# An RMS norm that streams 64 MB: three rows stored singly between pieces of a load, statistics one group ahead, and bulk transfers cut by partition

## The chip, the cores and the metric

The kernel runs on one core of a Trainium2 chip. A core has engines that work side by side: VectorE (DVE), ScalarE (ACT), TensorE (PE), GpSimd (POOL) and SyncE (SP), which here does nothing but issue transfers. Transfers between the chip's main memory (HBM) and the on-chip memory of 128 partitions (SBUF) are carried by 16 DMA engines. The metric is the time of one execution on the device in microseconds; the median over several runs is compared.

## The reference

The input `x` is 16 x 1024 rows of 512 fp32 numbers, 16,384 rows in all; `gamma` has 512 numbers.

```python
rms = np.sqrt(np.mean(x ** 2, axis=-1, keepdims=True) + 1e-5)
return (x / rms * gamma).astype(np.float32)
```

Every row is squared and averaged, and the row is then scaled by one number of its own and by `gamma`. So 33.5 MB are read and 33.5 MB are written, with little arithmetic for each number.

## The kernel before

The 16,384 rows are four tiles of 128 partitions x 32 rows x 512 numbers, 8 MB each (1 MB is 2^20 bytes in this text where tiles are spoken of; a tile is 64 KB in each partition). Row r of a tile in a partition lies beside row r+1 in HBM, so a partition's 32 rows are one contiguous piece. Three tiles fit in SBUF, as `slot0`, `slot1` and `slot2`. The fourth tile goes into `slot0` again, once the first tile has been stored from it. The results are written over the input in the slot and stored from there.

All large transfers are issued from SP in the order of the program: `load` is line 42 and `store` line 45. Each is one transfer over all 128 partitions. SP works through its list in order. Where a transfer must wait (a store for the arithmetic, a load for the store that frees its slot), SP waits, and all that stands behind it on SP waits too. Transfers that have been issued then stand in the queue of the DMA engines.

`compute` works on groups of eight rows (G = 8). There are two ways to get the sums of squares. In even groups ScalarE squares one row at a time and accumulates its sum (line 78, eight times). In odd groups ScalarE squares four rows at a time into PSUM (line 72) and VectorE sums these (line 73). Then ScalarE takes the root of eight means (line 84), VectorE the reciprocal (line 85), and VectorE scales each of the eight rows by its own number and by `gamma` (line 87). The order in which these instructions stand on each engine is made by a scheduler from the program, which mixes neighbouring groups.

The order of transfers on SP (lines 47 to 49, and lines 96 to 112): the first tile in two loads of 16 rows, the second tile in one load, then one single row of the first tile as a store, then the third tile in one load, the other 31 rows of the first tile, half of the second tile, the two halves of the fourth tile as loads into `slot0`, the other half of the second tile, the third tile, and the two halves of the fourth tile. The single-row store makes the load behind it on SP wait until that row has been computed.

Of the kernel before, what the change touches and what calls it, by code (L numbers as in the profile page):

```python
# [1 line left out]

# [4 lines left out]


@with_exitstack
def kernel(  # L10
    ctx: ExitStack,
    tc: tile.TileContext,
    x: bass.AP,
    gamma: bass.AP,
    out: bass.AP,
):
    nc = tc.nc
    P = nc.NUM_PARTITIONS
    eps = 1e-5
    fp32 = mybir.dt.float32  # L20
    AF = mybir.ActivationFunctionType
    OP = mybir.AluOpType

    xf = x.flatten_outer_dims()
    of = out.flatten_outer_dims()
    N, D = xf.shape
    R = 32
    G = 8
    H = 4
    assert N == 4 * P * R  # L30

    xv = xf.rearrange("(t p r) d -> t p r d", p=P, r=R)
    ov = of.rearrange("(t p r) d -> t p r d", p=P, r=R)

    const = ctx.enter_context(tc.tile_pool(name="const", bufs=1))
    stats = ctx.enter_context(tc.tile_pool(name="stats", bufs=4))
    psum = ctx.enter_context(tc.tile_pool(name="psum", bufs=2, space=bass.MemoryType.PSUM))

    slots = [const.tile([P, R, D], fp32, name=f"slot{i}") for i in range(3)]

    def load(t, slot, r0, r1):
        nc.sync.dma_start(out=slots[slot][:, r0:r1], in_=xv[t][:, r0:r1])

    def store(t, slot, r0, r1):
        nc.sync.dma_start(out=ov[t][:, r0:r1], in_=slots[slot][:, r0:r1])

    load(0, 0, 0, 16)
    load(0, 0, 16, 32)
    load(1, 1, 0, 32)

    gamma_row = const.tile([1, D], fp32)
    nc.scalar.dma_start(out=gamma_row, in_=gamma.unsqueeze(0))
    ones_col = const.tile([1, P], fp32)
    nc.vector.memset(ones_col, 1.0)  # L54
    gamma_psum = psum.tile([P, H, D], fp32, name="sq")
    nc.tensor.matmul(gamma_psum[:, 0], ones_col, gamma_row, start=True, stop=True)  # L56
    gamma_b = const.tile([P, D], fp32)
    nc.vector.tensor_copy(out=gamma_b, in_=gamma_psum[:, 0])  # L58

    eps_t = const.tile([P, 1], fp32)  # L60
    nc.vector.memset(eps_t, eps)  # L61
    sq_scratch = const.tile([P, D], fp32)

    def compute(slot, r0, r1):
        for g in range(r0, r1, G):
            ss = stats.tile([P, G], fp32, name="ss")
            rms = stats.tile([P, G], fp32, name="rms")
            rstd = stats.tile([P, G], fp32, name="rstd")
            if (g // G) % 2:
                for h in range(0, G, H):  # L70
                    sq = psum.tile([P, H, D], fp32, name="sq")
                    nc.scalar.activation(out=sq, in_=slots[slot][:, g + h : g + h + H, :], func=AF.Square)  # L72
                    nc.vector.tensor_reduce(  # L73
                        out=ss[:, h : h + H], in_=sq, axis=mybir.AxisListType.X, op=OP.add
                    )
            else:
                for r in range(G):
                    nc.scalar.activation(  # L78
                        out=sq_scratch,
                        in_=slots[slot][:, g + r, :],  # L80
                        func=AF.Square,
                        accum_out=ss[:, r : r + 1],
                    )
            nc.scalar.activation(out=rms, in_=ss, func=AF.Sqrt, bias=eps_t, scale=1.0 / D)  # L84
            nc.vector.reciprocal(out=rstd, in_=rms)  # L85
            for r in range(G):
                nc.vector.scalar_tensor_tensor(  # L87
                    out=slots[slot][:, g + r, :],
                    in0=slots[slot][:, g + r, :],
                    scalar=rstd[:, r : r + 1],  # L90
                    in1=gamma_b,
                    op0=OP.mult,
                    op1=OP.mult,
                )

    compute(0, 0, 8)
    store(0, 0, 0, 1)
    load(2, 2, 0, 32)
    compute(0, 8, 32)
    store(0, 0, 1, 32)  # L100
    compute(1, 0, 16)
    store(1, 1, 0, 16)
    load(3, 0, 0, 16)
    load(3, 0, 16, 32)
    compute(1, 16, 32)
    store(1, 1, 16, 32)
    compute(2, 0, 32)
    store(2, 2, 0, 32)
    compute(0, 0, 16)
    store(3, 0, 0, 16)  # L110
    compute(0, 16, 32)
    store(3, 0, 16, 32)


# [1 line left out]
_INS = ['x', 'gamma']  # L116
_OUTS = [((16, 1024, 512), 'float32')]


# [23 lines left out]
```

## Time and profile before

| What | Value |
|---|---|
| Median of 11 runs | 162.19 us (161.86 to 162.61) |
| The profiled execution's own time | 162.1 us |
| Its span (first to last instruction) | 160.3 us |
| VectorE busy | 123.4 us (77%), 163 instructions |
| ScalarE busy | 79.9 us (50%), 162 instructions |
| Scaling of rows, line 87 | 128 instructions, 744 ns each, 85.7 us |
| Sums from PSUM, line 73 | 16 instructions, 2274 ns each, 36.1 us |
| Squares by four rows, line 72 | 16 instructions, 1860 ns each, 29.8 us |
| Squares by one row, line 78 | 64 instructions, 625 ns each, 40.0 us |
| HBM read and written | 33.56 MB and 33.55 MB |

The page gives each engine's busy time, a row of 40 slices of the span with a digit for the busy share in tenths, the packets of each DMA queue with the time that they took as a share of 16 engines' span, the chain of work that ended last, and the waits. In an answer on waits the numbers are the total in microseconds, how often, and the longest. In the timeline the first number is the start in microseconds, the second the duration of the instruction; for an instruction that issues a transfer this is the issue alone. In an answer on DMA issues the last number is the median of the microseconds from issue to landing; where the answer covers one issue, it is that issue's own.

### The profile page before, as it was taken

To read this page: it belongs to the slowest core of one execution; us is meant where nothing else is said; L and a number is where in the kernel's file an instruction comes from. 1 tells how busy PE (TensorE), PEld (TensorE's weight loads), DVE (VectorE), ACT (ScalarE), POOL (GpSimd) and SP (SyncE) were. 2 spreads that over 40 slices of the span, in tenths; PEclk is the share of its full clock that TensorE was granted. 3 is DMA by queue.
4 is the path that set the end of the run, shared out by engine and by line. 5 is a ranking of instruction groups with operands and counts; after the bars stand their busy time and mean duration, and the time that the engine had idled before them with its cause. 6 is when DMAs were issued, how large, how long until landed. Compare 5 with 4: busy or idle time off the path is not lost.

```text
span 160.3 us, 404 instructions
## 1 busy us (share of the span) xinstructions
PE 2.0 (1%) x2; PEld 0.5 (0%) x2; DVE 123.4 (77%) x163; ACT 79.9 (50%) x162; POOL 0.2 (0%) x4
## 2 busy tenths in 40 slices
PE   4000000000000000000000000000000000000000
PEld 1000000000000000000000000000000000000000
DVE  0101909999999509999999999998999999998000
ACT  3008999930490999993089504002998970000000
POOL 0000000000000000000000000000000000000000
DMA  7999999969799895999899999999997997999993
GB/s 262 392 401 491 417 392 523 523 262 523 327 525 425 360 523 253 509 507 412 348 392 499 409 401 474 433 401 442 450 531 343 458 507 327 433 425 401 392 507 147
DMA packets 1876, 67.13 MB, mean 419 GB/s; under 512 B 209, under 2 KB 209, under 8 KB 338
## 3 DMA queue, kind: packets, MB, share of 16 engines
q1 hardware_dynamic: 1872, 67.11, 97.8%
q14 instruction: 2, 0.02, 0.0%
q10 hardware_dynamic: 2, 0.00, 0.0%
HBM read 33.56 MB, written 33.55 MB: 419 GB/s over the span
## 4 chain that ended last, share of the span: by engine, by line
DVE 71%; ACT 12%; DMA 8%; issue 1%; DVEq 0%
DVE slot L87 52%; DVE ss L73 18%; DMA slot<-in_x_dram 8%; ACT sq_scratch L78 6%; ACT sq L72 4%; DVE rstd L85 1%; ACT L84 1%; ACT rms L84 1%; DVEq L138 0%
## 5 line engine op out<-in xcount | busy, mean ns | idle before, releaser
L87 DVE SCALAR_TENSOR_TENSOR slot<-slot,rstd,gamma_b 128x512 f32<-128x512 f32 x128 | 85.7, 744 | 0.1
L78 ACT ACTIVATE sq_scratch<-slot 128x512 f32<-128x512 f32 x64 | 40.0, 625 | 14.4 <-DMA slot<-in_x_dram 13.0
L73 DVE TENSOR_REDUCE ss<-sq 128x4 f32<-128x2048 f32 x16 | 36.1, 2274 | 10.5 <-ACT sq L72 10.4
L72 ACT ACTIVATE sq<-slot 128x2048 f32<-128x2048 f32 x16 | 29.8, 1860 | 4.4 <-DVE ss L73 4.4
L84 ACT ACTIVATE rms<-ss,eps_t 128x8 f32<-128x8 f32 x16 | 4.4, 297 | 37.4 <-DVE ss L73 37.2
L78 ACT ACTIVATION_READ_ACCUMULATOR sq_scratch<-slot 128x1 f32 x64 | 11.9, 186 | 0.0
L85 DVE RECIPROCAL rstd<-rms 128x8 f32<-128x8 f32 x16 | 2.7, 187 | 9.8 <-ACT rms L84 9.8
L58 DVE COPY gamma_b<-sq 128x512 f32<-128x512 f32 x1 | 0.7, 691 | 3.2 <-PE sq L56 3.2
L56 PE MATMUL sq<-gamma_row,ones_col 1*128 1x512 f32 x2 | 2.0, 1122 | 2.1 <-DMA gamma_row<-in_gamma_dram 2.1
L78 ACT ACT_TABLE_LOAD x1 | 1.3, 1283 | 1.3 <-PEq L127 1.3
L84 ACT ACT_TABLE_LOAD x1 | 1.3, 1283 | 0.0
L54 DVE MEMSET ones_col<- 1x128 f32 x1 | 0.2, 165 | 0.8 <-PEq L127 0.8
L56 PEld LDWEIGHTS sq<-gamma_row,ones_col 1*128 1x128 f32 x2 | 0.5, 308 | 2.1 <-issue 2.1
L127 POOL MEMSET const-bfloat16-1.0<- 128x1 bf16 x1 | 0.1, 102 | 0.0
L127 POOL MEMSET const-uint8-127<- 128x1 uint8 x1 | 0.1, 102 | 0.0
L127 POOL MEMSET const-float32-0.0<- 128x1 f32 x1 | 0.1, 99 | 0.2 <-issue 0.2
L127 POOL MEMSET const-float32-1.0<- 128x1 f32 x1 | 0.1, 99 | 0.0
L61 DVE MEMSET eps_t<- 128x1 f32 x1 | 0.1, 59 | 0.0
## 6 DMA issues: line engine op xcount, KB each, us to landing
slot<-in_x_dram SPq DMA_DIRECT2D x4, 4096.0 KB, 21.3
out_dram<-slot SPq DMA_DIRECT2D x4, 4096.0 KB, 17.8
out_dram<-slot SPq DMA_DIRECT2D x1, 7936.0 KB, 31.6
out_dram<-slot SPq DMA_DIRECT2D x1, 256.0 KB, 18.2
slot<-in_x_dram SPq DMA_DIRECT2D x2, 39.0
gamma_row<-in_gamma_dram ACTq DMA_DIRECT2D x1, 2.0 KB
out_dram<-slot SPq DMA_DIRECT2D x1, 23.0
```

Source lines behind the costliest of these rows:

```text
L54: nc.vector.memset(ones_col, 1.0)
L56: nc.tensor.matmul(gamma_psum[:, 0], ones_col, gamma_row, start=True, stop=True)
L58: nc.vector.tensor_copy(out=gamma_b, in_=gamma_psum[:, 0])
L61: nc.vector.memset(eps_t, eps)
L72: nc.scalar.activation(out=sq, in_=slots[slot][:, g + h : g + h + H, :], func=AF.Square)
L73: nc.vector.tensor_reduce(out=ss[:, h : h + H], in_=sq, axis=mybir.AxisListType.X, op=OP.add)
L78: nc.scalar.activation(out=sq_scratch, in_=slots[slot][:, g + r, :], func=AF.Square, accum_out=ss[:, r : r + 1],)
L84: nc.scalar.activation(out=rms, in_=ss, func=AF.Sqrt, bias=eps_t, scale=1.0 / D)
L85: nc.vector.reciprocal(out=rstd, in_=rms)
L87: nc.vector.scalar_tensor_tensor(out=slots[slot][:, g + r, :], in0=slots[slot][:, g + r, :], scalar=rstd[:, r : r + 1], in1=gamma_b, op0=O ...
L127: nc = _bacc.Bacc("TRN2", target_bir_lowering=False, num_devices=1)
```

## The change

The transfers are cut in other pieces, and the arithmetic is put in another order.

- The first tile's first load of 16 rows becomes two loads of 8.
- `load` and `store` get an argument `parts`, which cuts a transfer into consecutive ranges of partitions, issued one after the other. The second tile's load and the first tile's large store are cut in two (64 partitions each), the third tile's store in four (32 partitions each).
- The load of the third tile, which came in one piece behind the single-row store, now comes in three pieces (16, 8 and 8 rows), with a store of one more single row of the first tile between each two. The large store of the first tile begins at row 3.
- `compute` is divided into `row_stats` (squares, sums, root, reciprocal) and `apply` (scaling). The loop calls `row_stats` of the next group before `apply` of this one.

```diff
-    def load(t, slot, r0, r1):
-        nc.sync.dma_start(out=slots[slot][:, r0:r1], in_=xv[t][:, r0:r1])
+    def load(t, slot, r0, r1, parts=1):
+        for p in range(0, P, P // parts):
+            q = slice(p, p + P // parts)
+            nc.sync.dma_start(out=slots[slot][q, r0:r1], in_=xv[t][q, r0:r1])
...
+    def store(t, slot, r0, r1, parts=1):
+        for p in range(0, P, P // parts):
+            q = slice(p, p + P // parts)
+            nc.sync.dma_start(out=ov[t][q, r0:r1], in_=slots[slot][q, r0:r1])
...
-    load(0, 0, 0, 16)
+    load(0, 0, 0, 8)
+    load(0, 0, 8, 16)
     load(0, 0, 16, 32)
-    load(1, 1, 0, 32)
+    load(1, 1, 0, 32, parts=2)
...
+    def transfers(t, g):
+        if (t, g) == (0, 0):
+            store(0, 0, 0, 1)
+            load(2, 2, 0, 16)
+            store(0, 0, 1, 2)
+            load(2, 2, 16, 24)
+            store(0, 0, 2, 3)
+            load(2, 2, 24, 32)
+        elif (t, g) == (0, 24):
+            store(0, 0, 3, 32, parts=2)
+        elif (t, g) == (1, 8):
+            store(1, 1, 0, 16)
+            load(3, 0, 0, 16)
+            load(3, 0, 16, 32)
+        elif (t, g) == (1, 24):
+            store(1, 1, 16, 32)
+        elif (t, g) == (2, 24):
+            store(2, 2, 0, 32, parts=4)
+        elif (t, g) == (3, 8):
+            store(3, 0, 0, 16)
+        elif (t, g) == (3, 24):
+            store(3, 0, 16, 32)
+
+    ahead = row_stats(0, 0)
+    for k, (t, g) in enumerate(groups):
+        rstd = ahead
+        if k + 1 < len(groups):
+            tn, gn = groups[k + 1]
+            ahead = row_stats(slot_of[tn], gn)
+        apply(slot_of[t], g, rstd)
+        transfers(t, g)
```

## The prediction

> **What bounds the kernel now.** I read the page's chain first, then the DMA rows and the queue totals, then the waits of SP, and last the time of issue and the landing of each transfer.
>
> ```profile
> DVE 71%; ACT 12%; DMA 8%; issue 1%; DVEq 0%
> DMA  7999999969799895999899999999997997999993
> DMA packets 1876, 67.13 MB, mean 419 GB/s; under 512 B 209, under 2 KB 209, under 8 KB 338
> q1 hardware_dynamic: 1872, 67.11, 97.8%
> SPq L45 <- DVE slot L87: 122.4, 7, 28.3
> SPq L42 <- DMA out_dram<-slot: 8.2, 1, 8.2
> ```
>
> The chain puts 71% on VectorE, but the packets of SP's queue occupy 97.8% of sixteen DMA engines' span. Both can't be the bound. SP's waits for VectorE, 122.4 us in seven places, only delay the time at which a store joins the queue. Whether that costs anything is decided by what the queue still holds then. So here are five transfers with issue time (timeline) and time from issue to landing (DMA issues, asked around each issue):
>
> ```profile
> 25.23 0.44 SPq L42 DMA_DIRECT2D slot<-in_x_dram  x1
> 50.08 0.34 SPq L45 DMA_DIRECT2D out_dram<-slot  x1
> 117.02 0.34 SPq L45 DMA_DIRECT2D out_dram<-slot  x1
> 132.58 0.33 SPq L45 DMA_DIRECT2D out_dram<-slot  x1
> 147.88 0.33 SPq L45 DMA_DIRECT2D out_dram<-slot  x1
> ```
>
> ```profile
> slot<-in_x_dram SPq DMA_DIRECT2D x1, 37.4
> out_dram<-slot SPq DMA_DIRECT2D x1, 7936.0 KB, 31.6
> out_dram<-slot SPq DMA_DIRECT2D x1, 23.0
> out_dram<-slot SPq DMA_DIRECT2D x1, 4096.0 KB, 17.1
> out_dram<-slot SPq DMA_DIRECT2D x1, 4096.0 KB, 11.5
> ```
>
> Row by row: 25.23+37.4 = 62.6 is the landing of the third tile's load; 50.08+31.6 = 81.7 of the first tile's store; 117.02+23.0 = 140.0 of the third tile's store; 132.58+17.1 = 149.7 and 147.88+11.5 = 159.4 of the fourth tile's stores. The same sum for the others gives 12.8 and 22.5 (first tile), 42.3 (second tile, issued 1.64, 40.7 later), 43.0 (the single row, issued 24.84), 91.5 and 120.7 (second tile's stores) and 111.0 (fourth tile's load). Neighbouring landings differ by what a transfer needs at the rate of the bulk: 19.8, 19.6, 19.1, 19.3 us for 8 MB (the third is 7.75 MB), 9.7 us for 4 MB. And each store was issued before the queue had come to it: 50.08 against 62.6 (12.5 us spare), 117.02 against 120.7 (3.7), 147.88 against 149.7 (1.8). The queue is never empty. The kernel is bound by the DMA engines; VectorE, with 123.4 us busy, is second and has slack everywhere. The chain names it because that last store waited for it, without showing the 1.8 us of queue behind it.
>
> What can be won is small. The slope of 19.3 us for 8 MB over 64 MB is 154.4 us. The span has 160.3. The other 5.9 us are the start (the first 4 MB land at 12.8, 9.7 of it slope), the last 0.9 us after 159.4, and less than 2 us at changes of direction and the single row.
>
> [...] The trace of before agrees with the full rate: 8 MB in 19.3 us is 435 GB/s. It has no bulk transfer of fewer than 128 partitions, so the half rate isn't shown[...].
>
> **The change part by part.** Arithmetic first: 128 scalar_tensor_tensor, 16 tensor_reduce, 16 reciprocals, all squares and roots are the same in number and shape; only their order moves. Cost 0, hidden behind the queue.
>
> First load in parts: the first 8 rows (2 MB) land at about 8.0 instead of 12.8, as the first 4 MB took 9.7 us. ScalarE needed 12.81 to 22.14 for the eight row squares and two large squares ahead of the root, then the first row was out at 24.84. With an earlier start by 4.8 us it is out near 20. Its store isn't due before the second tile has landed, at 42.3, so nothing is gained. One more DMA issue on SP, 0.4 us at the start, comes after transfers that already run: 0.
>
> Statistics one group ahead: VectorE reduces the next group before it scales this one. The group that pays is the last one scaled before a store, at most two reduces (2 x 2274 ns) later, 4.5 us; after the queue has fallen behind as below, every store has more spare time than that. Cost 0. If the queue kept its rate, the stores with 3.7 and 1.8 us spare would be the ones to watch, but a group that is put ahead also has its reduces done when its own scaling starts, so the end of VectorE's total doesn't move.
>
> Three rows stored singly, between three pieces of the third tile's load: the single row now takes 42.3 to 43.0, 0.7 us, against 19.1/31 = 0.62 in bulk. Two more rows leave the bulk, 2 x 0.08, and there are four more changes of direction, bounded by 0.35 us at 62.6 to 81.7 (19.1 against 31 x 0.604 = 18.7). Bounds 0.1 to 1.4; I take 0.3. On SP the pieces wait behind row 1 and row 2, each 0.7 us of VectorE later, some 20 us before they are due. The waits for reused DMA semaphores name the first loads (landed by 22.5) and, for the two halves of the first store, the halves of the second tile's load. These land before the third tile's load begins, so the halves are still in the queue early: 0.
>
> The split by partition is the part that decides. Three bulk transfers lose half their partitions: the second tile's load (22.5 to 42.3: 19.8 us, now two of 64), the first tile's store without three rows (29/31 of 19.1 = 17.9, two of 64) and the third tile's store (120.7 to 140.0: 19.3, four of 32). Queue order puts the halves one after the other[...]. Lower bound: each packet keeps its rate, extra 0 (a gain is looked at below). Upper bound: exactly half the rate, extra 57.0. [...] I take 54.5[...].
>
> Is there cover for it? No: the queue is full from start to end. Does anything late add to it? The second tile lands near 61 (22.5 + 2 x 19.4), the third near 83, the first store ends near 118, only then are the two loads of the fourth tile issued, behind 9.7 us of the second tile's first store, which was ready at about 82 (the tile's landing plus some 20 us, half a tile's arithmetic and a wait): covered. Those loads land near 138 and 148, the second tile's other store near 157, the third tile's store near 195, the last two near 205 and 215. VectorE needs 123.4/4 = 31 us per tile: third tile ready at about 130, due at 157; fourth about 166, due at 205. No new hole.
>
> Sum against the profiled execution: 160.3 + 54.5 + 0.3 = 215.1 us of span; the run of this profile took 162.1, 1.8 more than its span and 0.1 under the median 162.19. So 216.9, taken as **217.0 us**.
>
> **Rivals.** First, the split costs nothing[...]. Then span 160.3 + 0.3, time 162.4 (162.1 to 163.5). For it: no transfer of before has fewer partitions, so nothing in the profile excludes it. [...]
>
> Second, only one direction is limited, loads (write to SBUF) or stores: 162.1 + 19.8 + 0.3 = 182.2, or 162.1 + 37.2 + 0.3 = 199.6. Engines drifting apart, so that some are in the other half already, would land between these too. Against it: landings follow each other as one queue, and no row of before tells the directions apart.
>
> Third, it gets faster. Place: the end of each transfer[...]. It needs the half rate to be absent and the row cost near its lower bound. The price is in the less than 2 us of changes; half of it is 0.8 us, time 161.4. It decides from 0.4 us of gain onward, more than the rows take. Against: nothing in the page shows an engine waiting.
>
> **How the numbers follow.** Half rate both ways 0.72 (212 to 221), one direction or drift 0.10 (182 to 210), no cost 0.14, faster 0.04. Of the 0.14, 0.06 lie within 0.2% (161.87 to 162.51, about what a measurement of this kernel tells from no change) and 0.08 above. So faster 0.04, same 0.06, slower 0.90. The range from 180 to 222 leaves out the last two cases, 0.18.
>
> **What would show it.** Right: packets of SP's queue 15 x 128 + 2 x 64 + 2 x 64 + 4 x 32 and 16 small ones for each of 23 transfers, 2672 in all (before: 13 x 128 + 13 x 16 = 1872); their time still near 97% of the engines; the GB/s row near 215 in three stretches (22 to 61, 83 to 118, 157 to 195) and near 430 elsewhere; landings as listed; mean near 312 GB/s. Half rate wrong: no slow stretch, second tile at 42.3. One direction: one or two of the three. Hole: a DMA digit well under 9 inside the span, and a store issued later than the landing ahead of it. What makes the forecast wrong above all is the split of 64 rows over the engines, of which before shows nothing.

## The result, and the profile after

The changed kernel takes 221.33 us (median of 12 runs, 220.01 to 223.54) against 162.30 us for the kernel before (46 runs). The ratio is 1.3626, with a 95% interval from 1.3599 to 1.3653; ratios in this text leave out executions more than 1.5% above the fastest of their kernel, here one of the twelve. The profiled execution took 220.04 us with a span of 218.3 us, 58.0 us more than before.

First the page of the changed kernel: the DMA rows in 40 slices of 5.5 us, the packets, and SP's queue.

```profile
span 218.3 us, 425 instructions
DMA  6999999999969999889995999999999899979993
GB/s 250 432 471 420 348 192 192 192 192 192 192 276 446 393 431 486 174 174 261 218 218 252 420 354 408 450 396 426 474 276 204 192 252 192 216 204 426 426 432 144
DMA packets 2676, 67.13 MB, mean 308 GB/s; under 512 B 369, under 2 KB 369, under 8 KB 754
q1 hardware_dynamic: 2672, 67.11, 97.8%
```

The DMA engines are as busy as before, 97.8% of the span, with the same 67.11 MB. There is no hole that would explain 58 us. But in three stretches, slices 6 to 11, 17 to 22 and 31 to 36, the second row shows about 200 GB/s where the rest shows about 430. A busy share alone hides this: it is 97.8% here as before, at 308 GB/s for 419, since an engine counts as busy for the whole of a packet, however slowly the packet moves. Bytes and busy share must be read together.

The packets show it more sharply. These are the totals of SP's queue in a stretch of the second tile's load: before from 24 to 41 us, then after from 25 to 60 us, each with packets of 64 KB (after has 16 of a few bytes beside them). The columns are packets, MB, and time of the packets as a share of 16 engines' stretch; a packet's whole time counts where it starts, so a share can pass 100%.

```profile
q1 hardware_dynamic: 112, 7.34, 102.3%
```

```profile
q1 hardware_dynamic: 128, 7.34, 101.9%
```

Before, 112 large packets take 1.023 x 16 x 17 us, 2.48 us each (2.42 once such a load is under way, as a cut of it shows below). After, the same 112 packets and 7.34 MB take 1.019 x 16 x 35 us, 5.1 us each. The work on the queue is the same; each packet takes a little more than twice as long.

Next the issue times of the changed kernel's transfers (timeline of SP, asked around each), and the time from issue to landing in the same order. In the first fence the first row holds five issues, of which the two halves of the second tile's load are the last.

```profile
0.72 2.56 SPq L44 DMA_DIRECT2D slot<-in_x_dram  x5
45.85 0.51 SPq L49 DMA_DIRECT2D out_dram<-slot  x1
63.32 0.50 SPq L49 DMA_DIRECT2D out_dram<-slot  x1
160.22 0.35 SPq L49 DMA_DIRECT2D out_dram<-slot  x1
175.36 0.35 SPq L49 DMA_DIRECT2D out_dram<-slot  x1
```

```profile
slot<-in_x_dram SPq DMA_DIRECT2D x1, 60.6
out_dram<-slot SPq DMA_DIRECT2D x1, 3712.0 KB, 54.6
out_dram<-slot SPq DMA_DIRECT2D x1, 3712.0 KB, 55.7
out_dram<-slot SPq DMA_DIRECT2D x1, 4096.0 KB, 47.5
out_dram<-slot SPq DMA_DIRECT2D x1, 4096.0 KB, 42.1
```

The second half of the second tile's load, issued at 2.7, lands at 63.3; the halves of the first tile's store at 100.4 and 119.0; the last two stores at 207.8 and 217.4. Each of the last two stores takes over 40 us from issue to landing, of which 9.6 us are the transfer itself (217.4 - 207.8); the kernel before had 11.5 us for the last one. The arithmetic is now far from the end of the span. From differences of landings, on both sides counted to the last engine's:

| Stretch of the queue | Before, us | After, us | More |
|---|---|---|---|
| up to the first tile's landing | 22.5 | 23.0 | 0.5 |
| second tile's load (split in 2) | 19.8 | 40.3 | 20.5 |
| single rows and third tile's load | 20.3 | 22.1 | 1.8 |
| rest of the first tile's store (split in 2; two rows less) | 19.1 | 33.6 | 14.5 |
| second tile's stores, fourth tile's loads | 39.0 | 40.4 | 1.4 |
| third tile's store (split in 4) | 19.3 | 38.7 | 19.4 |
| fourth tile's stores | 19.4 | 19.3 | -0.1 |
| sum | 159.4 | 217.4 | 58.0 |

Two rows moved from the fourth line to the third, some 1.2 us. Then the three split transfers hold 20.5 + 15.7 + 19.4 = 55.6 us of the 58.0.

The chain of waits misleads here too. For the changed kernel it begins so:

```profile
another core or an unknown queue 26%; DVE 24%; ACT 16%; DMA 13%; issue 1%; DVEq 0%; SPq 0%; ACTq 0%
```

There is one core, and its queue is known. SP's own waits are of more use: its stores waited 46.4 us for loads (10.7 before), and the end of the program 41.5 us for stores (11.0 before). First the two lines of the kernel before, then those of the changed kernel:

```profile
SPq L138 <- DMA out_dram<-slot: 11.0, 2, 9.6
SPq L45 <- DMA slot<-in_x_dram: 10.7, 1, 10.7
```

```profile
SPq L49 <- DVE slot L94: 74.1, 5, 25.6
SPq L49 <- DMA slot<-in_x_dram: 46.4, 4, 19.8
SPq L162 <- DMA out_dram<-slot: 41.5, 5, 10.3
SPq L44 <- DMA out_dram<-slot: 29.1, 2, 18.5
```

### The profile page after: what moved, and what is told of

It reads as the page before. It is cut to its first block, busy times and chain, and to the rows that moved or that the text cites. A ratio compares the mean times of both kernels' runs of the same rounds, so it can differ in the third digit from the quotient of the medians.

```text
span 218.3 us, 425 instructions
## 1 busy us (share of the span) xinstructions
PE 2.0 (1%) x2; PEld 0.5 (0%) x2; DVE 123.1 (56%) x163; ACT 80.1 (37%) x162; POOL 0.2 (0%) x4
## 3 DMA queue, kind: packets, MB, share of 16 engines
q1 hardware_dynamic: 2672, 67.11, 97.8%
## 4 chain that ended last, share of the span: by engine, by line
another core or an unknown queue 26%; DVE 24%; ACT 16%; DMA 13%; issue 1%; DVEq 0%; SPq 0%; ACTq 0%
DVE slot L94 19%; DMA slot<-in_x_dram 13%; ACT sq_scratch L82 9%; ACT sq L76 6%; DVE ss L77 5%; DVE rstd L89 1%; ACT rms L88 1%; DVEq L162 0%; SPq L49 0%; SPq L44 0%; ACTq L82 0%
```

## The experiments

Theory, from the prediction: a transfer that names only one half of the partitions (0 to 63 or 64 to 127, or 32 of these) moves at about half the rate, in both directions. This was an estimate of the author's, as no transfer of before is of this kind; in the changed kernel such packets took 5.1 us for 2.48. The traces show packets, bytes and times, but not what slows a packet, so the theory is tested by which partitions a transfer names. Rivals: the order of work opens holes; any transfer with fewer rows is slow; one direction alone is; the limit lies on the side of HBM, since half a tile's partitions are also half a tile's addresses.

### Which part of the change costs

**The changed kernel without the split.**

```diff
-    load(1, 1, 0, 32, parts=2)
+    load(1, 1, 0, 32)
...
-            store(0, 0, 3, 32, parts=2)
+            store(0, 0, 3, 32)
...
-            store(2, 2, 0, 32, parts=4)
+            store(2, 2, 0, 32)
```

> The changed kernel with every transfer over all 128 partitions again; the rows between the load's pieces, the first load in parts and the statistics one group ahead stay. [...]the split carries nearly all of the 59 us, so 163.2 us (162.4 to 164.0); what is left over is about 0.5 us for two more single rows and 0.5 us for the start. Rival (order of work: statistics ahead or the waits on SP for reused semaphores open holes in the queue): over 167 us, and a DMA digit under 9 inside the span.

162.36 us against 162.04, ratio 1.0023 (1.0014 to 1.0031), just under the range expected. So the split carries 221.33 - 162.36 = 59.0 us, and all the rest of the change 0.3. The queue's share is 97.7%, and no slice inside the span falls lower than in before. The order of work is out as a cause of the loss.

**The rows alone, on the kernel before.**

```diff
     store(0, 0, 0, 1)
-    load(2, 2, 0, 32)
+    load(2, 2, 0, 16)
+    store(0, 0, 1, 2)
+    load(2, 2, 16, 24)
+    store(0, 0, 2, 3)
+    load(2, 2, 24, 32)
...
-    store(0, 0, 1, 32)
+    store(0, 0, 3, 32)
```

> The kernel before with the three single rows between three pieces of the third tile's load, and nothing else. Theory: two more rows of 2 KB packets and four more changes of direction cost 0.5 us, time 162.8 (162.4 to 163.4). Rival (hidden: the rows would have been stored anyway): within 0.1 us of before. Rival (SP issues the pieces late, and the queue runs dry): over 164.

162.07 against 162.00, ratio 1.0000 (0.9989 to 1.0012), under the range expected: the rival "hidden" was right, and 0.5 us was too much. The rows don't slow the queue by anything that can be measured.

**First load in parts and statistics ahead alone**: the changed kernel with the split undone as above, and the rows too.

```diff
             store(0, 0, 0, 1)
-            load(2, 2, 0, 16)
-            store(0, 0, 1, 2)
-            load(2, 2, 16, 24)
-            store(0, 0, 2, 3)
-            load(2, 2, 24, 32)
+            load(2, 2, 0, 32)
...
-            store(0, 0, 3, 32)
+            store(0, 0, 1, 32)
```

> The changed kernel without the split by partition and without the two further rows: what is left is the first load in two parts and the statistics one group ahead. Theory: both hidden by the full queue, 162.3 (162.0 to 162.8), at most 0.5 us more at the start. Rival (the arithmetic's order matters at the end, where the last store had 1.8 us to spare): the last store is issued after 149.7 us of the span, and the time is over 163.

162.19 against 162.00, ratio 1.0004 (0.9993 to 1.0015). The trace shows what happened to the arithmetic:

```profile
20.58 0.35 SPq L49 DMA_DIRECT2D out_dram<-slot  x1
...
83.25 59.67 SPq L49 DMA_DIRECT2D out_dram<-slot  x4
```

The first row is out at 20.58 instead of 24.84, and the last store is issued at the end of the second row, 83.25 + 59.67 = 142.9, instead of 148.2 (both are the end of the issue). So the results are ready earlier, by 4 us at the start and 5 at the end, and all of it is spent waiting in the queue.

**The kernel before without its single row.**

```diff
-    store(0, 0, 0, 1)
     load(2, 2, 0, 32)
...
-    store(0, 0, 1, 32)
+    store(0, 0, 0, 32)
```

> The kernel before without its single-row store: the first tile is stored in one transfer of 32 rows, and the third tile's load is issued at the start. Theory: one row less in small packets and two changes of direction less save 0.1 to 0.5 us, time 162.0 (161.7 to 162.2). Rival: the queue moves the same bytes and nothing changes, 162.3.

A miss: 162.60 against 162.00, ratio 1.0036 (1.0022 to 1.0051). The loss is small but clear of the noise, and a gain or nothing was expected. There are fewer transfers and the same bytes, but the third tile's store and the last one take longer to land, 23.8 us for 23.0 and 12.3 for 11.5, from issue times within 0.1 us of before's. The third tile's load, now directly behind the second's, is where the spread between the sixteen engines first grows (landings from 61.8 to 63.1, in before from 62.2 to 62.6). Why an engine falls behind there isn't settled.

### One transfer split, one direction at a time

In this section and the next ones `load` and `store` have an argument `cuts`, the list of partitions between which a transfer is cut; its definition is left out of the diffs.

**The second tile's load in two halves.**

```diff
...
-    load(1, 1, 0, 32)
+    load(1, 1, 0, 32, cuts=(0, 64, 128))
```

> The kernel before with the second tile's load alone as two transfers of 64 partitions. [...]both halves at half rate, packets of 64 KB about 5.1 us instead of 2.42, the load 40.3 us instead of 19.8, time 162.3 + 20.5 = 182.8 (181 to 184). Rival stores only (writing to SBUF isn't limited): 162.5. Rival drift (the long run loses more or less because engines fall out of step): 175 to 180.

182.65 against 162.04, ratio 1.1266 (1.1247 to 1.1284): 20.6 us more, as expected.

**The third tile's store in four quarters.**

```diff
...
-    store(2, 2, 0, 32)
+    store(2, 2, 0, 32, cuts=(0, 32, 64, 96, 128))
```

> The kernel before with the third tile's store alone as four transfers of 32 partitions. [...]the store takes 38.7 us instead of 19.3, time 162.3 + 19.4 = 181.7 (180 to 183). Rival loads only: 162.5. Rival that the number of partitions sets the rate (32 of 128 is a quarter): 57 us more, 219.

183.24 against 162.04, ratio 1.1302 (1.1278 to 1.1325): 21.2 us more, just above the range expected. So both directions are limited, and cuts of 32 partitions cost what cuts of 64 do (21.2 us more on a store of 19.3, 20.6 on a load of 19.8). That the rate goes with the number of partitions as such is out: it would have cost 57 us.

### Fewer rows, or the wrong rows

**The load cut at 32 and 96.**

```diff
...
-    load(1, 1, 0, 32)
+    load(1, 1, 0, 32, cuts=(0, 32, 96, 128))
```

> The kernel before with the second tile's load as partitions 0 to 31, 32 to 95 and 96 to 127. The middle one has 64 partitions and the same packets as a half of the changed kernel, but 32 of each side of partition 64. [...]the middle transfer runs at the full rate, packets of 2.42 us, 9.7 us; the outer ones at half, 2 packets of 5.1 us per engine each, 10.2 us; together 30.1 instead of 19.8, time 172.6 (171.5 to 174). Rival (any transfer of 64 partitions or fewer is slow, by the number of its partitions or its shorter list for each engine): all three at half, 40 us, time 182.8, and no packets of 2.42 us in that stretch.

171.94 against 162.04, ratio 1.0602 (1.0586 to 1.0619), 9.9 us more. The three parts of the load in this kernel, issued at 1.62, 2.10 and 2.72 us, with their time to landing:

```profile
slot<-in_x_dram SPq DMA_DIRECT2D x1, 31.3
slot<-in_x_dram SPq DMA_DIRECT2D x1, 40.9
slot<-in_x_dram SPq DMA_DIRECT2D x1, 50.2
```

They land at 32.9, 43.0 and 52.9, after the first tile at 22.6. So 32 partitions (2 MB) take 10.3 us, the middle 64 (4 MB) 10.1, and 32 again 9.9. The queue's total from 33.5 to 41 us, inside the middle part, has 48 large packets and nothing else:

```profile
q1 hardware_dynamic: 48, 3.15, 96.8%
```

0.968 x 16 x 7.5 us / 48 = 2.42 us each. The transfer of partitions 32 to 95 runs at the full rate, and each neighbour of half its size takes as long. Which partitions, not how many: the rival of fewer rows is out.

**Even and odd partitions.**

```diff
-    load(1, 1, 0, 32)
+    for p in range(2):
+        nc.sync.dma_start(out=slots[1][p:P:2], in_=xv[1][p:P:2])
```

> The kernel before with the second tile's load as two transfers of 64 partitions, even ones and odd ones. [...]half rate, 182.8 (178 to 184). Rival [...]162.5. In between, 165 to 178, if the engines fall out of step and stay so.

161.93 against 162.00, ratio 0.9993 (0.9982 to 1.0004). The half rate, named first, fell; its rival was right: 64 partitions ran at the rate of 128 when every second one was named. The engines had not fallen out of step: in the DMA row from 24 to 41 us, in 40 slices of 0.425 us, the packets start together about every 2.4 us.

```profile
DMA  9700099000099000097000990000990000990000
```

Why this cut costs nothing isn't shown. The eight transfers of 16 partitions below test whether only the half counts in which the partitions lie. The run also shows that two transfers of 64 partitions cost nothing as such.

### Which side of the transfer

**One half of SBUF, addresses all over the tile in HBM.**

```diff
-    load(1, 1, 0, 32)
+    nc.sync.dma_start(out=slots[1][0:64], in_=xv[1][0:P:2])
+    nc.sync.dma_start(out=slots[1][64:128], in_=xv[1][1:P:2])
...
-    store(2, 2, 0, 32)
+    nc.sync.dma_start(out=ov[2][0:P:2], in_=slots[2][0:64])
+    nc.sync.dma_start(out=ov[2][1:P:2], in_=slots[2][64:128])
```

> The kernel before with the second tile's load and the third tile's store each in two transfers: SBUF partitions 0 to 63 with the even 64 KB blocks of the tile in HBM, 64 to 127 with the odd ones. (The rows of these two tiles so land in other places of the output; the work is the same.) Each transfer has one half of SBUF's partitions and addresses from all over the tile in HBM. Theory SBUF side: half rate in both, 20.3 and 19.4 us more, 202 (199 to 205). Rival HBM side (in the changed kernel a half is also a contiguous half of 8 MB of HBM): 162.5. If the load is limited on one side and the store on the other: about 182.

203.44 against 162.07, ratio 1.2557 (1.2530 to 1.2584): 41.4 us more, in the range of the theory.

**Both halves of SBUF, one half of the tile's addresses in HBM.**

```diff
-    load(1, 1, 0, 32)
+    nc.sync.dma_start(out=slots[1][0:P:2], in_=xv[1][0:64])
+    nc.sync.dma_start(out=slots[1][1:P:2], in_=xv[1][64:128])
...
-    store(2, 2, 0, 32)
+    nc.sync.dma_start(out=ov[2][0:64], in_=slots[2][0:P:2])
+    nc.sync.dma_start(out=ov[2][64:128], in_=slots[2][1:P:2])
```

> The counterpart: the same two tiles in two transfers each, even SBUF partitions with the first contiguous 4 MB of the tile in HBM, odd ones with the second. (Again the rows of these tiles land elsewhere.) Theory SBUF side: 162.3, packets of 2.42 us throughout. Rival HBM side: 202. One side for the load and the other for the store: about 182.

162.23 against 162.07, ratio 1.0010 (0.9998 to 1.0022). The queue's totals in the load, of the first kernel from 25 to 60 us, of the second from 24 to 41 us:

```profile
q1 hardware_dynamic: 128, 7.34, 102.0%
```

```profile
q1 hardware_dynamic: 128, 7.34, 100.5%
```

The same 7.34 MB need 35 us in the one and 17 us in the other. The limit is on the side of SBUF, for the load and for the store (one of them alone would have left some 182 us in both kernels). HBM is out.

### A half, or a smaller part

**Eight transfers of 16 partitions**, for the second tile's load and the third tile's store.

```diff
...
-    load(1, 1, 0, 32)
+    load(1, 1, 0, 32, cuts=range(0, 129, 16))
...
-    store(2, 2, 0, 32)
+    store(2, 2, 0, 32, cuts=range(0, 129, 16))
```

> The kernel before with the second tile's load and the third tile's store each in eight transfers of 16 partitions. [...]a quarter of the rate, 8 MB in some 78 us instead of 19.5, 58 us more for each of the two, 279 (265 to 290), packets near 10 us. Rival halves (only the side of partition 64 counts, as the even-odd cut[...] ran at full rate): 20 us more for each, 202, packets of 5.1 us.

260.61 (median of four, 258.1 to 262.7) against 162.07. The ratio, 1.5940 (1.5896 to 1.5983), is that of the two runs near 258 us; the trace is of the longest, 262.7. The total was outside the range named (265 to 290), but it is far from the rival's 202. The load does what was expected; the queue from 24 to 94 us:

```profile
DMA packets 224, 7.34 MB, mean 105 GB/s; under 512 B 112, under 2 KB 112, under 8 KB 112
q1 hardware_dynamic: 224, 7.34, 93.5%
```

112 large packets, 0.935 x 16 x 70 us / 112 = 9.35 us each, nearly four times the 2.42. The load takes 74.5 us (landings 23.2 to 97.7) for 19.8. So there is more than a half at work: 16 partitions in a row get about a quarter of the rate. With that, a limit that knows only two halves is out; how the even and odd partitions escape it stays open. The store takes 65.3 us instead of 77 (landings 175.2 to 240.5). In its landing events the first of the sixteen engines has finished the eighth part at 204.1 us and the last at 240.5: engines fall out of step, and those ahead are already in other parts. Its packets begin at 7 to 9.4 us each and later range from 2.4 to 13. Its 12 us under 77 are most of the 18 us by which the expectation was too high.

**Two halves at the same time from two lists.**

```diff
-    store(2, 2, 0, 32)
+    nc.sync.dma_start(out=ov[2][0:64], in_=slots[2][0:64])
+    nc.scalar.dma_start(out=ov[2][64:128], in_=slots[2][64:128])
```

> The kernel before with the third tile's store in two halves of 64 partitions, the first issued from SP, the second from ScalarE, at the same time. [...]nearly the half rate, 178 to 182. Rival out of step: [...]162 to 170; ScalarE's wait ahead of its transfer may then delay the fourth tile's squares by some 6 us, of which the queue has 7 to spare for the next store.

175.22 against 162.07, between both expectations. The four times, from 172.05 to 177.91, lie too far apart for a ratio. In the profiled execution (172.05 us) the issues around 117 us have this time to landing:

```profile
out_dram<-slot SPq DMA_DIRECT2D x1, 33.0
out_dram<-slot ACTq DMA_DIRECT2D x1, 33.1
```

The queue of ScalarE from 117 to 150 us:

```profile
q10 hardware_dynamic: 80, 4.19, 37.0%
```

Its 64 large packets (the other 16 are of a few bytes) take 0.370 x 16 x 33 us / 64 = 3.05 us each, between the 2.42 of the full rate and the 5.1 of a half. Issued at 117.1, both transfers land near 150.1. In before the single transfer landed at 140.0. Ten microseconds are lost instead of nineteen, and the queue is not empty before the last stores (landings 159.7 and 169.4; the last was issued at 157.4). Why these packets are slowed less than those of one half alone isn't shown. An uncut transfer is better by 10 to 16 us of the whole.

## Why the prediction was right

The forecast was 217.0 us with a range from 180 to 222; 221.33 was measured, near the upper end.

**The bound.** That the queue, not VectorE, sets the time was right. The clearest proof is the kernel without the split and the rows: its arithmetic was done 5 us earlier and its time was 1.0004 of before's.

**The split.** The forecast held in each point that the runs test: about half the rate for one half of the partitions (packets of 5.1 us), both directions (20.6 us more for the load alone, 21.2 for the store alone), one half after the other (the load's halves landed at 43.1 and 63.3), and no cover. What the partitions of a half have in common was not shown. The size was off by little. The step took 54.5 us, the author's estimate, a little under exact halving (57.0); no trace of before shows it. Of the profile's 58.0 us, 55.6 lie in the split transfers. Exact halving was no upper bound for the load: 40.3 us is 2.04 times 19.8, since a packet takes 5.1 us where twice 2.42 would be 4.84. The estimate had taken 54.5 / 57.0 = 0.96 of halving, and the load has 20.5 / 19.8 = 1.04. The store of the first tile was cheaper than halving, 15.7 for 17.9 us. Its packets (58 KB) show where. From 101.3 to 110.5 us, in the second half, 32 of them and nothing else give 1.006 x 16 x 9.2 / 32 = 4.63 us each:

```profile
q1 hardware_dynamic: 32, 1.90, 100.6%
```

But each engine's first packet, started from 83.3 to 84.9 us directly behind the third tile's load, took only 2.2 to 2.4 us. This alone saves 2.4 us on each engine; why these packets were not slowed isn't known. So the total came close to the forecast in part by luck: the load took 0.7 us more than halving and this store 2.2 us less, and neither was foreseen.

**The rest of the gap.** 218.3 of span against 215.1 is 3.2 us: 1.1 in the split transfers (55.6 for 54.5), 1.4 in the stretch behind the first store, and the rest at the start and the rows, where 0.3 was taken and 0.5 + 0.6 - 0.1 was read. The 1.4 us lie in packets of 32 KB, some of which took up to 2.4 us instead of 1.21, nearly all of them between 124 and 131 us and between 144 and 147, near the changes from store to load and back; the cause is open. Another 1.3 us separate the profiled execution (220.04) from the median.

**First load in parts, statistics ahead.** Cost 0, right: ratio 1.0004. The first row came out at 20.55 in the changed kernel, where "near 20" was forecast. **Three rows.** 0.3 us was more than this shows by itself: 1.0000. All three edits together cost 0.3 us (1.0023).

**No new hole.** Right: 97.8% of the engines' time, 2672 packets as counted ahead, and each landing came 1 to 3 us later than listed.

**The rivals.** No cost of the split: out, by the changed kernel itself. One direction: out, by the load alone (+20.6) and the store alone (+21.2). Faster: out; no variant here beat the kernel before, and the four that came closest have ratios whose intervals include 1. Its place, the spread between engines at a transfer's end, is real, though: without the single row this spread grew from 0.4 to 1.3 us at the third tile's load and the kernel lost 0.36%.

## What to carry to other kernels

A transfer's rate depended here on which partitions it named: packets of 64 KB took 2.42, 5.1 or 9.35 us. Cut a large one along rows within the partition (1.0000 in this case), or not at all. If it must be cut by partition, take every second partition (0.9993). Partitions 32 to 95 ran at the full rate too (2.42 us), but the parts left over at 0 to 31 and 96 to 127 did not (10.3 and 9.9 us for 2 MB), and that cut cost 6%. When the DMA engines are busy all the time, compare bytes with busy time by stretch, since an engine on a slow packet counts as busy: 97.8% before and after, at 419 and 308 GB/s. And ask of every edit to the arithmetic how long its result then waits in the queue; 5 us won ahead of a full queue were worth nothing.

## What was not expected

With one half of the partitions a little more than half the rate is lost: packets of 64 KB took 5.1 us against 2.42. With sixteen they took 9.35, a little less than four times as long. The first packets of the first tile's store, right behind a load, were hardly slowed at all (2.2 to 2.4 us for 58 KB). Even and odd partitions ran at the full rate (0.9993), although sixteen partitions in a row ran at about a quarter; why stays open. And taking away one small store between two loads cost 0.36%, for a reason not found.
